# Three PEER query tiles computed from tokens x weight, with 1/rms applied to their scores

## The chip, the cores and the metric

The kernel runs on one core of a Trainium2 chip. The metric is the device time of one execution in microseconds (us). The engines named below are TensorE (PE, with its weight loads as PEld), VectorE (DVE), ScalarE (ACT), GpSimd (POOL) and SyncE (SP, which here issues most of the DMAs). Each engine works off its own list of instructions in order, and waits on semaphores for the others.

## The reference, cut to what matters

Two transformer blocks are applied to 256 tokens of width 1024. The first has two gated feed-forward parts around a token mixer; the second has a hybrid mixer, a cross attention to 256 memory tokens, and a PEER feed-forward part, after which the result is normalised. All is float32. What the change touches is the start of the PEER part:

```python
def rmsnorm_2(x, w):
    y = x * lax.rsqrt(jnp.mean(x * x, axis=-1, keepdims=True) + NORM_EPS)
    return y * w
...
x = x + memory_cross_attention(...)
x = x + peer_ffn(rmsnorm_2(x, norm_ffn_w), peer_wq, peer_sub_keys, peer_u, peer_v)
...
def peer_ffn(h, wq, sub_keys, u_table, v_table):
    q = (hf @ wq).reshape(t, PEER_HEADS, 2, PEER_HALF)        # 8 heads x 2 halves = 16 query tiles of 128
    sc = jnp.einsum('thpd,hpnd->thpn', q, sub_keys)           # 128 scores per token and tile
    top_v, top_i = lax.top_k(sc, PEER_TOPK)                   # the 16 best of each
    ... 16 best pairs of each head, softmax, and for the chosen experts gelu(u . h) times v
```

The kernel takes u . h for all 16,384 experts (128 tiles of 128, here called `pu`), and lets the gates choose.

## The kernel before, in words

Activations are kept transposed, as eight tiles of 128 features x 256 tokens: `hT` is the residual stream. A product in float32 is made of three fast products: weight and activation are each split into a rounded high part and the rest, and high x high, high x low and low x high are summed in PSUM. So each weight tile of 128x1024 (512 KB) goes through four steps in `Weights.chunk`: a DMA from SP into `raw` (L264), a cast on ACT into `whi` (L265), a subtraction on DVE that leaves `wlo` (L266), and 24 matmuls of 128x256 on PE (L192, the line of the helper that all matmuls share). `raw` has three buffers, `whi` and `wlo` two in each pool; in the PEER stage every third tile puts both parts into `wpair` instead (L266 there too), which takes over the place of `hT`.

The part in question runs as follows.

- The cross attention (`xa`) ends in its output projection, eight tiles of 24 matmuls on the moving operands `xoh` and `xol`; `ev_o` adds each to its part of `hT` (DVE, L1148).
- `norm_u` (L1154) then normalises: ACT squares each part of `hT` (L351), DVE adds the squares into `sqa` (L353), two matmuls with `mean` give the mean square of each token (`sm`), ACT takes the root (L362, with a table load ahead), DVE the reciprocal (L364), and `spread` makes of it a 128x256 tile that is the same on every partition: DVE writes two diagonal matrices `rd` (L372), PE multiplies them with ones. Then for each of eight parts DVE makes `nz` = hT x weight x 1/rms (L392), ACT casts it into `uh` (L273) and DVE leaves the rest in `ul` (L274).
- With `uh` and `ul` PE computes the sixteen query tiles (`pq`) and the first 24 of the 128 `pu` tiles, two query tiles and three `pu` tiles in turn (`weave`). `ev_q` takes a query tile out of PSUM into `qt` (ACT, L1206), loads its 128 keys (`ky`, SP, L1204), and computes the scores of the query tile before it (`scores`): two float32 matmuls of 128x128, a copy into `s1_` (ACT, L1219), and `top16` on DVE for each half of the tokens: MAX, MAX_INDEX, MATCH_REPLACE, MAX, MAX_INDEX (L1194 to L1198), ten instructions in all for a query tile.
- 36 `pu` tiles follow beside the choice of the pairs (`picks`), 68 beside the gates, and at last 128 steps with the `pv` tiles, where the weight tile is the moving operand in 512 columns.

A scheduler puts the instructions of each engine in one fixed order, by the order in which they were written and by its own estimate of when their inputs come; the pools set how far ahead a tile can be loaded. Small tiles called `edge` in the code place large tiles at chosen addresses; the pool `cp` lies ahead of all others in SBUF.

Of the kernel before, what the change touches and what calls it, by code (L numbers as in the profile page):

```python
# [12 lines left out]
F32 = mybir.dt.float32  # L13
F32R = mybir.dt.float32r
I32 = mybir.dt.int32
U32 = mybir.dt.uint32
AF = mybir.ActivationFunctionType
# [5 lines left out]
P = 128  # L23
T = 256
D = 1024
KD = 8
# [3 lines left out]
EPS = 1e-6  # L30
NEG = -1.0e30
NEXP = 128


_COLS = [
# [150 lines left out]
def body(tc, A, out):  # L186
    nc = tc.nc
    es = ExitStack()
    dve, act, pe, gp, sp = nc.vector, nc.scalar, nc.tensor, nc.gpsimd, nc.sync
# [4 lines left out]
    cp = es.enter_context(tc.tile_pool(name="cp", bufs=1))  # L194
# [18 lines left out]
    def col(name, j):  # L213
        o = _COFF[name][0] + j
        return cols[:, o:o + 1]
# [16 lines left out]
    def new_u():  # L232
        if first:
            return first.pop()
        return (cp.tile([P, KD, T], F32R, name="uh", tag="uh"),
                cp.tile([P, KD, T], F32R, name="ul", tag="ul"))
# [39 lines left out]
    def linear(*a):  # L276
        for _ in linear_steps(*a):
            pass
# [20 lines left out]
    def linear_steps(w, KT, ms, xh, xl, evac):  # L299

        per = 8 // KT if KT < 8 else 1
        for m0 in range(0, len(ms), per):
            grp = ms[m0:m0 + per]
            pss = [pmm.tile([P, 512], F32, name="mm", tag="mm") for _ in grp]
            for k0 in range(0, KT, 8):
                kn = min(8, KT - k0)
                if per > 1:
                    hi, lo = W.chunk(w[grp[0] // per], (per * KT, P))
                else:
                    hi, lo = W.chunk(w[grp[0], :, k0:k0 + kn, :], (kn, P))  # L310
                for g, m in enumerate(grp):
                    ps = pss[g][:, :T]
                    for k in range(kn):
                        kk = k0 + k
                        wh, wl = hi[:, g * KT + k, :], lo[:, g * KT + k, :]
                        mm(ps, wh, xh[:, kk, :], start=(kk == 0), stop=False)
                        mm(ps, wh, xl[:, kk, :], start=False, stop=False)
                        mm(ps, wl, xh[:, kk, :], start=False, stop=(kk == KT - 1))
            for g, m in enumerate(grp):
                evac(m, pss[g][:, :T])  # L320
            yield
# [24 lines left out]
    def sum_sq(pool, src, w=None):  # L346

        acc = pool.tile([P, T], F32, name="sqa", tag="sqa", bufs=2)
        for k in range(KD):
            sq = acc if k == 0 else pool.tile([P, T], F32, name="sq", tag="sq", bufs=2)  # L350
            act.activation(sq, src[:, k, :], AF.Square, scale=1.0 if w is None else w(k))  # L351
            if k:
                dve.tensor_tensor(acc, acc, sq, OP.add)  # L353
        ps = psm.tile([P, 512], F32, name="sm", tag="sm")
        for t in range(2):
            mm(ps[:, t:t + 1], acc[:, t * P:(t + 1) * P], mean)
        return ps[:, 0:2]

    def rsqrt(pool, ms):

        r = pool.tile([P, 2], F32, name="rr", tag="rr", bufs=4)
        act.activation(r, ms, AF.Sqrt, bias=epsc)  # L362
        r2 = pool.tile([P, 2], F32, name="rr2", tag="rr2", bufs=4)
        dve.reciprocal(r2, r)  # L364
        return r2

    def spread(pool, r):

        ps = psm.tile([P, 512], F32, name="sm", tag="sm")
        for t in range(2):  # L370
            d = pool.tile([P, P], F32, name="rd", tag="rd", bufs=2)
            dve.tensor_scalar(d, ident, r[:, t:t + 1], None, OP.mult)  # L372
            mm(ps[:, t * P:(t + 1) * P], ones, d)
        return ps[:, :T]

    def norm_u(pool, src, hi, lo, a, b):

        norm_apply(pool, src, spread(pool, rsqrt(pool, sum_sq(pool, src))), hi, lo, a, b)

    def scale_u(src, hi, lo, a):  # L380

        for k in range(KD):
            act.activation(hi[:, k, :], src[:, k, :], AF.Copy, scale=a(k))
            dve.scalar_tensor_tensor(lo[:, k, :], src[:, k, :], a(k), hi[:, k, :].bitcast(F32),
                                     OP.mult, OP.subtract)

    def norm_apply(pool, src, r, hi, lo, a, b):

        for k in range(KD):
            z = pool.tile([P, T], F32, name="nz", tag="nz", bufs=2)  # L390
            if b is None:
                dve.scalar_tensor_tensor(z, src[:, k, :], a(k), r, OP.mult, OP.mult)  # L392
            else:
                dve.tensor_tensor(z, src[:, k, :], r, OP.mult)
                z2 = pool.tile([P, T], F32, name="nz2", tag="nz2", bufs=2)
                act.activation(z2, z, AF.Identity, scale=a(k), bias=b(k))
                z = z2
            split(hi[:, k, :], lo[:, k, :], z)
# [706 lines left out]


    with tc.tile_pool(name="xa", bufs=1) as xp_:
        xK = xp_.tile([P, KD, T], F32, name="xK")
        xV = xp_.tile([P, 2, D], F32, name="xV")
        sp.dma_start(xK, kd)  # L1110
        sp.dma_start(xV, vd)

        uh, ul = new_u()
        scale_u(hT, uh, ul, lambda k: col("nxa", k))
        rq = rsqrt(npool, sum_sq(npool, hT))
        dve.tensor_scalar(rq, rq, 1.0 / 16.0, None, OP.mult)
        xq = xp_.tile([P, KD, T], F32, name="xq")
        edge(xp_, 192)
        xoh = xp_.tile([P, KD, T], F32R, name="xoh")
        xol = xp_.tile([P, KD, T], F32R, name="xol")  # L1120

        def attend(h):
            pst = [psm.tile([P, 512], F32, name="sm", tag="sm") for _ in range(2)]
            for t in range(2):
                ps = psm.tile([P, 512], F32, name="sm", tag="sm")
                for e in range(2):
                    mm(ps[:, :T], xq[:, 2 * h + e, t * P:(t + 1) * P], xK[:, 2 * h + e, :], start=(e == 0), stop=(e == 1))
                lg = xp_.tile([P, T], F32, name="xlg", tag="xlg", bufs=2)
                act.activation(lg, ps[:, :T], AF.Copy, scale=rq[:, t:t + 1])
                softmax_rows(xp_, lg, T, "x")  # L1130
                for kt in range(2):
                    pe.transpose(pst[kt][:, t * P:(t + 1) * P], lg[:, kt * P:(kt + 1) * P], ident)
            pt = xp_.tile([P, 2, T], F32, name="xpt", tag="xpt", bufs=2)
            for kt in range(2):
                act.copy(pt[:, kt, :], pst[kt][:, :T])
            for e in range(2):
                ps = psm.tile([P, 512], F32, name="sm", tag="sm")
                o = h * 256 + e * P
                for kt in range(2):
                    mm(ps[:, :T], xV[:, kt, o:o + P], pt[:, kt, :], start=(kt == 0), stop=(kt == 1))  # L1140
                split(xoh[:, 2 * h + e, :], xol[:, 2 * h + e, :], ps[:, :T])

        for h in range(4):
            linear(A["xa_q"], KD, [2 * h, 2 * h + 1], uh, ul, lambda m, ps: act.copy(xq[:, m, :], ps))
            attend(h)

        def ev_o(m, ps):
            dve.tensor_tensor(hT[:, m, :], ps, hT[:, m, :], OP.add)  # L1148

        linear(A["xa_o"], KD, list(range(8)), xoh, xol, ev_o)  # L1150


    uh, ul = new_u()
    norm_u(npool, hT, uh, ul, lambda k: col("nffn", k), None)  # L1154
    hd = dr.tile([P, KD, T], F32, name="hd")
    act.dma_start(hd, hT)
    W.pools = [wa]
# [29 lines left out]
    with tc.tile_pool(name="sel", bufs=1) as sp_:  # L1187
# [2 lines left out]

        def top16(s, v, ix, n):

            s2 = sp_.tile([P, n], F32, name="s2", tag=f"s2{n}", bufs=2)
            dve.max(v[:, 0:8], s)  # L1194
            dve.max_index(ix[:, 0:8], v[:, 0:8], s)
            dve.match_replace(s2, v[:, 0:8], s, -3.0e38)
            dve.max(v[:, 8:16], s2)
            dve.max_index(ix[:, 8:16], v[:, 8:16], s2)  # L1198
# [11 lines left out]
        def scores():  # L1210

            if not queries:
                return
            m, qt, ky = queries.pop()
            sc = psm.tile([P, 512], F32, name="sm", tag="sm")
            for t in range(2):
                mm(sc[:, t * P:(t + 1) * P], qt[:, t * P:(t + 1) * P], ky)
            s = sp_.tile([P, T], F32, name="s1_", tag="s1_", bufs=3)
            act.copy(s, sc[:, :T])  # L1219
            for t in range(2):  # L1220
                top16(s[:, t * P:(t + 1) * P], tv[t][:, m, :], ti[t][:, m, :], P)

# [78 lines left out]
                yield from pick_steps(t)  # L1301

        def q_steps():
            yield from linear_steps(A["pq"], KD, list(range(16)), uh, ul, ev_q)
            scores()

        weave(q_steps(), u_steps(0, NU1, u_ev), 2, 3)
# [92 lines left out]
```

## Time and profile before

| what | value |
|---|---|
| runs | 1742.51 us median of 3 (1738.4 to 1745.0) |
| profiled execution | 1747.64 us, of it a span of 1745.9 us from the first to the last instruction |
| mean granted TensorE clock | 0.990 of full speed |
| PE busy | 1679.2 us, 96% of the span |
| DVE busy | 1253.2 us, 72% |
| ACT busy | 1023.6 us, 59% |

Times inside the execution count from the start of the span. The kernel spends it in a chain of stages in which PE has little idle time; the transition from cross attention to PEER lies at 905 to 920 us, and the PEER part fills all that follows.

### The profile page before, as it was taken

What the parts mean: (1) busy time and instruction counts of PE and PEld (TensorE: products, weight loads), DVE (VectorE), ACT (ScalarE), POOL (GpSimd) and SP (SyncE); (2) the same over time, 40 slices, a digit from 0 to 9 for tenths busy, and PEclk for the clock granted to TensorE, in tenths of its full rate; (3) what the DMA queues carried; (4) which work ended last, traced back from release to release, by engine and by line L of the source; (5) the groups of instructions that cost most, each with busy time, mean ns of one, the idle gap of its engine ahead of it and who ended that gap; (6) DMA issues with size and microseconds to landing.
All of it is one profiled execution on the core that took longest, in us unless ns stands there. A gap on an engine that the chain in (4) does not pass through costs nothing.

```text
span 1745.9 us, 31700 instructions
## 1 busy us (share of the span) xinstructions
PE 1679.2 (96%) x12298; PEld 1575.6 (90%) x12298; DVE 1253.2 (72%) x2223; ACT 1023.6 (59%) x1977; POOL 4.0 (0%) x36
## 2 busy tenths in 40 slices
PE   2999999899999999899999999999999999999998
PEld 2998998799999999898889999999999888888886
DVE  7888677767855579757557789589999755555554
ACT  5655466565744458666645446588877544445444
POOL 0000000000000000000000000000000000000000
PEclk9999999999999999999999999999999999999999
DMA  9988689345866657216425555644444555555554
GB/s 334 342 307 312 204 291 326 122 134 184 288 205 191 182 185 234 87 38 209 142 76 191 183 180 174 203 145 146 145 135 143 190 193 195 194 174 192 195 194 138
DMA packets 97717, 336.34 MB, mean 193 GB/s; under 512 B 10988, under 2 KB 16541, under 8 KB 96926
## 3 DMA queue, kind: packets, MB, share of 16 engines
q1 hardware_dynamic: 94828, 330.63, 56.2%
q10 hardware_dynamic: 2738, 3.68, 0.6%
q8 instruction: 97, 1.59, 0.4%
q14 instruction: 54, 0.44, 0.1%
HBM read 329.02 MB, written 5.25 MB: 191 GB/s over the span
## 4 chain that ended last, share of the span: by engine, by line
PE 78%; DVE 12%; ACT 4%; issue 3%; DMA 2%; SPq 0%; DVEq 0%; ACTq 0%
PE mm L192 71%; PE sm L192 7%; DVE wlo L266 3%; DVE aw L1329 2%; ACT whi L265 1%; DMA wr<-in_w_ada 1%; DVE ac L820 1%; DVE wr L430 0%; DMA mnr<-in_rows 0%; DVE aw L1185 0%; DVE at L664 0%; DVE wpair L266 0%; DVE ul L274 0%; DMA xaV<-ke 0%; DVE ch L1285 0%
## 5 line engine op out<-in xcount | busy, mean ns | idle before, releaser
L266 DVE TENSOR_TENSOR wlo<-raw,whi 128x1024 fp32r<-128x1024 f32 (+1 forms) x448 | 543.1, 1214 | 250.5 <-ACT whi L265 249.9
L265 ACT CAST whi<-raw 128x1024 fp32r<-128x1024 f32 (+1 forms) x448 | 465.8, 1042 | 383.1 <-PE mm L192 270.1
L192 PE MATMUL mm<-uh,whi 128*128 128x256 f32 x2064 | 583.8, 285 | 9.8 <-ACT whi L265 7.4
L192 PE MATMUL mm<-ul,whi 128*128 128x256 f32 x2064 | 579.3, 281 | 2.7 <-DVE ul L274 2.2
L192 PE MATMUL mm<-uh,wlo 128*128 128x256 f32 x2064 | 578.3, 281 | 0.3 <-DVE wlo L266 0.2
L192 PEld LDWEIGHTS mm<-uh,whi 128*128 128x128 f32 x2064 | 391.4, 190 | 12.2 <-ACT whi L265 8.2
L192 PEld LDWEIGHTS mm<-ul,whi 128*128 128x128 f32 x2064 | 394.1, 191 | 4.4 <-DVE ul L274 2.7
L192 PEld LDWEIGHTS mm<-uh,wlo 128*128 128x128 f32 x2064 | 391.7, 190 | 2.1 <-DVE wlo L266 1.6
L266 DVE TENSOR_TENSOR wpair<-raw,wpair 128x1024 fp32r<-128x1024 f32 x90 | 110.2, 1224 | 80.6 <-ACT wpair L265 80.6
L192 PE MATMUL mm<-uh,wpair 128*128 128x256 f32 x768 | 143.8, 282 | 2.0 <-DVE wpair L266 1.7
L192 PE MATMUL mm<-whi,wh 128*128 128x512 f32 x344 | 134.0, 391 | 1.9 <-ACT wh L273 1.9
L192 PE MATMUL mm<-whi,wl 128*128 128x512 f32 x344 | 134.6, 391 | 0.0
L192 PE MATMUL mm<-wlo,wh 128*128 128x512 f32 x344 | 134.5, 391 | 0.0
L265 ACT CAST wpair<-raw 128x1024 fp32r<-128x1024 f32 x90 | 94.5, 1050 | 66.4 <-PE mm L192 65.3
L192 PEld LDWEIGHTS mm<-uh,wpair 128*128 128x128 f32 x768 | 119.9, 188 | 2.8 <-DVE wpair L266 2.3
L192 PE MATMUL mm<-wpair,wh 128*128 128x512 f32 x336 | 110.3, 389 | 0.0
L192 PE MATMUL mm<-ul,wpair 128*128 128x256 f32 x384 | 106.9, 278 | 0.0
L192 PE MATMUL mm<-hh,whi 128*128 128x256 f32 x352 | 99.2, 282 | 0.0
L192 PE MATMUL mm<-hl,whi 128*128 128x256 f32 x352 | 99.1, 282 | 0.0
L192 PE MATMUL mm<-hh,wlo 128*128 128x256 f32 x352 | 98.9, 281 | 0.0
L430 DVE SCALAR_TENSOR_TENSOR wr<-wr,cb 128x1024 f32<-128x1024 f32 x72 | 87.5, 1221 | 15.8 <-DMA wr<-in_w_ada 15.5
L192 PEld LDWEIGHTS mm<-whi,wh 128*128 128x128 f32 x344 | 64.6, 188 | 15.4 <-ACT wh L273 2.1
(838 smaller groups left out, 2631.7 us busy)
## 6 DMA issues: line engine op xcount, KB each, us to landing
raw<-in_pu SPq DMA_DIRECT2D x128, 512.0 KB, 3.3
raw<-in_pv SPq DMA_DIRECT2D x128, 512.0 KB, 3.3
raw<-in_ff_gu SPq DMA_DIRECT2D x88, 512.0 KB, 4.4
wr<-in_w_ada SPq DMA_DIRECT2D x72, 512.0 KB, 6.0
raw<-in_in_fm SPq DMA_DIRECT2D x34, 512.0 KB, 4.2
raw<-in_ff_dn SPq DMA_DIRECT2D x32, 512.0 KB, 3.7
raw<-in_in_tm SPq DMA_DIRECT2D x24, 512.0 KB, 4.9
raw<-in_in_gab SPq DMA_DIRECT2D x16, 512.0 KB, 3.7
```

What stands on the lines that cost most here:

```text
L192: pe.matmul(o, l, r, start=start, stop=stop)
L265: act.copy(hi[:, :n], raw[:, :n])
L266: dve.tensor_tensor(lo[:, :n], raw[:, :n], hi[:, :n].bitcast(F32), OP.subtract)
L430: dve.scalar_tensor_tensor(wr, wr, 1.0, cb, OP.mult, OP.mult, accum_out=mod[:, j:j + 1])
L820: dve.scalar_tensor_tensor(ac, xp[:, i:i + T], w(i), ac, OP.mult, OP.add)
L1329: dve.tensor_tensor(av[:, :, :nu], pv[:, :, :nu], av[:, :, :nu], OP.mult)
```

## The change

Three of the sixteen query tiles (`NQ0 = 3`) no longer wait for the norm. While the sum of squares is taken, `scale_u` writes `qh` and `ql`, the split of hT x weight without 1/rms: for each of the eight parts an ACT instruction (L384 after) and a DVE instruction (L385 after). They lie where the keys and values of the cross attention were (tags `xK` and `xV`). The first three `pq` tiles are multiplied with them. A copy of 1/rms is kept in a new tile `rc` (DVE, L1159 after), and the scores of these tiles are multiplied with it when they leave PSUM, in two ACT instructions of 128 columns in place of one of 256. The norm then follows as before for the other thirteen query tiles and all `pu` tiles. `ev_q` of the three early tiles stands first in `q_steps`. The scratch tile of `top16` has one tag for both of its widths. Lines after the first edit are one higher in the changed kernel, those of `top16` and later more.

```diff
+NQ0 = 3
...
-        xK = xp_.tile([P, KD, T], F32, name="xK")
-        xV = xp_.tile([P, 2, D], F32, name="xV")
+        xK = xp_.tile([P, KD, T], F32, name="xK", tag="xK")
+        xV = xp_.tile([P, 2, D], F32, name="xV", tag="xV")
...
-    uh, ul = new_u()
-    norm_u(npool, hT, uh, ul, lambda k: col("nffn", k), None)
+
+        qh = xp_.tile([P, KD, T], F32R, name="qh", tag="xK")
+        ql = xp_.tile([P, KD, T], F32R, name="ql", tag="xV")
+        scale_u(hT, qh, ql, lambda k: col("nffn", k))
+        rc = cp.tile([P, 2], F32, name="rc")
+        dve.tensor_copy(rc, rsqrt(npool, sum_sq(npool, hT)))
+        early = []
+        linear(A["pq"], KD, list(range(NQ0)), qh, ql, lambda m, ps: early.append((m, ps)))
+        uh, ul = new_u()
+        norm_apply(npool, hT, spread(npool, rc), uh, ul, lambda k: col("nffn", k), None)
...
-            s2 = sp_.tile([P, n], F32, name="s2", tag=f"s2{n}", bufs=2)
+            s2 = sp_.tile([P, P], F32, name="s2", tag="s2", bufs=2)[:, :n]
...
-            act.copy(s, sc[:, :T])
+            if m < NQ0:
+                for t in range(2):
+                    act.activation(s[:, t * P:(t + 1) * P], sc[:, t * P:(t + 1) * P], AF.Copy, scale=rc[:, t:t + 1])
+            else:
+                act.copy(s, sc[:, :T])
...
-            yield from linear_steps(A["pq"], KD, list(range(16)), uh, ul, ev_q)
+            for m, ps in early:
+                ev_q(m, ps)
+            yield from linear_steps(A["pq"], KD, list(range(NQ0, 16)), uh, ul, ev_q)
```

The lists of instructions are the same up to the transition. There, PE before goes from the last tile of the cross attention's projection (moving operand `xoh`) straight to the matmuls of the norm and then to the first query tiles on `uh`:

```order
L192 MATMUL mm_10521<-xoh_9867,wlo_10524 128x256
L192 MATMUL sm_10579<-mean_75,sqa_10556 128x1 x2
L192 MATMUL sm_10586<-rd_10587,ones_73 128x128
L192 MATMUL sm_10586<-rd_10590,ones_73 128x128
L192 MATMUL mm_10645<-uh_10554,whi_10647 128x256
L192 MATMUL mm_10680<-uh_10554,whi_10682 128x256
```

In the changed kernel 24 matmuls of the first early tile (mm_10603) and four of the second (mm_10634) stand between that projection and the mean:

```order
L193 MATMUL mm_10603<-qh_10553,wlo_10606 128x256
L193 MATMUL mm_10634<-qh_10553,whi_10636 128x256
L193 MATMUL mm_10634<-ql_10554,whi_10636 128x256
L193 MATMUL mm_10634<-qh_10553,wlo_10637 128x256
L193 MATMUL mm_10634<-qh_10553,whi_10636 128x256
L193 MATMUL sm_10595<-mean_75,sqa_10572 128x1 x2
L193 MATMUL mm_10634<-ql_10554,whi_10636 128x256
```

The rest of the second and the third early tile (mm_10665) follow, and only then the spreading of 1/rms, the first two scores, and the fourth and fifth query tile (mm_10806, mm_10859) on `uh`:

```order
L193 MATMUL mm_10665<-qh_10553,wlo_10668 128x256
L193 MATMUL sm_10698<-rd_10699,ones_73 128x128
L193 MATMUL sm_10698<-rd_10702,ones_73 128x128
L193 MATMUL sm_10766<-ky_10758,qt_10760 128x128 x2
L193 MATMUL sm_10788<-ky_10762,qt_10764 128x128 x2
L193 MATMUL mm_10806<-uh_10696,whi_10808 128x256
L193 MATMUL mm_10859<-uh_10696,whi_10861 128x256
L193 MATMUL mm_10806<-ul_10697,whi_10808 128x256
```

So three query tiles moved ahead of the norm on PE. On DVE, the split of the first `pu` tile (wpair_10734) before stands right behind the last `ul`, and the first `top16` behind three such splits:

```order
L274 TENSOR_TENSOR ul_10555<-nz_10617,uh_10554 128x256
L274 TENSOR_TENSOR ul_10555<-nz_10621,uh_10554 128x256
L266 TENSOR_TENSOR wpair_10734<-raw_10733,wpair_10734 128x1024
L266 TENSOR_TENSOR wlo_10766<-raw_10764,whi_10765 128x1024
L266 TENSOR_TENSOR wlo_10798<-raw_10796,whi_10797 128x1024
L1194 MAX tv0_10641<-s1__10718 128x8
```

In the changed kernel the last `ul` is followed by `top16` instructions; 34 of them, of the four query tiles with the scores s1__10769, s1__10791, s1__10844 and s1__10897, stand in one row, of which these are the first five:

```order
L275 TENSOR_TENSOR ul_10697<-nz_10733,uh_10696 128x256
L1209 MAX_INDEX ti0_10756<-tv0_10754,s2_10772 128x8
L1205 MAX tv1_10755<-s1__10769 128x8
L1205 MAX tv0_10754<-s1__10791 128x8
L1206 MAX_INDEX ti1_10757<-tv1_10755,s1__10769 128x8
L1207 MATCH_REPLACE s2_10778<-tv1_10755,s1__10769 128x128
```

At the end of that row comes the split of the first `pu` tile (now wpair_10913), and those of the next two between the last `top16` instructions:

```order
L1206 MAX_INDEX ti1_10757<-tv1_10755,s1__10897 128x8
L1209 MAX_INDEX ti0_10756<-tv0_10754,s2_10899 128x8
L1207 MATCH_REPLACE s2_10905<-tv1_10755,s1__10897 128x128
L267 TENSOR_TENSOR wpair_10913<-raw_10912,wpair_10913 128x1024
L1208 MAX tv1_10755<-s2_10905 128x8
L267 TENSOR_TENSOR wlo_10945<-raw_10943,whi_10944 128x1024
L1209 MAX_INDEX ti1_10757<-tv1_10755,s2_10905 128x8
L267 TENSOR_TENSOR wlo_10977<-raw_10975,whi_10976 128x1024
```

So on DVE the split has moved behind the choice of the best sixteen of four tiles. PE comes to the products with that split after the last matmuls of the fifth query tile (mm_10859) and a few of the first three `pu` tiles (mm_10911, mm_10942, mm_10974):

```order
L193 MATMUL mm_10859<-uh_10696,wlo_10862 128x256
L193 MATMUL sm_10894<-ky_10837,qt_10839 128x128 x2
L193 MATMUL mm_10911<-uh_10696,wpair_10913 128x256
L193 MATMUL mm_10911<-ul_10697,wpair_10913 128x256
L193 MATMUL mm_10942<-uh_10696,whi_10944 128x256
L193 MATMUL mm_10942<-ul_10697,whi_10944 128x256
L193 MATMUL sm_11040<-ky_10890,qt_10892 128x128 x2
L193 MATMUL mm_10974<-uh_10696,whi_10976 128x256
L193 MATMUL mm_10974<-ul_10697,whi_10976 128x256
L193 MATMUL mm_10911<-uh_10696,wpair_10913 128x256 x2
```

The tenth row is the first that reads the split. Apart from the order, `rc` takes 32 bytes of each partition in the pool `cp`, behind `uh` and `ul`, and every tile of the other pools begins 32 bytes further in the built program: `whi` at 55,648 where it was at 55,616, the `xoh` of the cross attention at 134,976 where it was at 134,944, the operand of the first feed-forward part's second product at 174,880 where it was at 174,848. `hT`, `uh` and `ul` stay.

## Rows read from the trace of the kernel before

**Rows 1.** The page: busy time of the engines (busy us, share of the span, instructions).

```profile
PE 1679.2 (96%) x12298; PEld 1575.6 (90%) x12298; DVE 1253.2 (72%) x2223; ACT 1023.6 (59%) x1977; POOL 4.0 (0%) x36
```

**Rows 2.** Busy time by windows from behind the transition to the end: the window, its length, then busy time and instructions of PE, PEld, DVE, ACT and POOL, the granted clock of PE (1.00 is 2.4 GHz, 0.50 is 1.2 GHz), DMA share and GB/s.

```profile
925.00:1040.00 115.00, 115.00 (x989) 115.00 (x988) 83.26 (x291) 55.74 (x93) 0.00 (x0) 1.00 0.55 183
1040.00:1060.00 20.00, 20.00 (x178) 20.00 (x177) 19.93 (x88) 12.91 (x18) 0.00 (x0) 1.00 0.55 182
1060.00:1100.00 40.00, 38.72 (x332) 37.92 (x331) 37.68 (x127) 24.62 (x37) 0.00 (x0) 1.00 0.57 187
1100.00:1380.00 280.00, 279.26 (x2426) 278.17 (x2424) 245.47 (x335) 208.36 (x545) 0.00 (x0) 1.00 0.44 149
1390.00:1740.00 350.00, 348.72 (x1555) 289.02 (x1553) 196.98 (x255) 172.03 (x260) 0.00 (x0) 1.00 0.56 186
```

**Rows 3.** Timeline of PE at the transition: start, duration, what, and in brackets the idle time before it and what ended it.

```profile
905.14 0.28 PE L192 MATMUL mm<-xoh,wlo 128*128 128x256 f32 x1
907.00 0.58 PE L192 MATMUL sm<-mean,sqa 128*128 128x1 f32 x4 [1.58 <-DVE sqa L353]
908.63 1.19 PE L192 MATMUL sm<-rd,ones 128*128 128x128 f32 x4 [1.06 <-DVE rd L372]
910.83 0.58 PE L192 MATMUL mm<-uh,whi 128*128 128x256 f32 x1 [1.01 <-ACT uh L273]
```

**Rows 4.** What PE waited for from 905 to 1110 us: us in total, times, longest.

```profile
PE sm L192 <- DVE sqa L353: 1.6, 1, 1.6
PE sm L192 <- DVE rd L372: 1.1, 1, 1.1
PE mm L192 <- ACT uh L273: 1.0, 1, 1.0
PE mm L192 <- DVE wpair L266: 1.0, 2, 0.8
PE mm L192 <- ACT whi L265: 0.5, 1, 0.5
```

**Rows 5.** Busy time of PE alone by windows, with its granted clock: the transition, and the stretches behind three longer waits of PE.

```profile
706.00:714.00 8.00, 6.76 (x23) 0.57 0.33 112
839.40:843.00 3.60, 3.48 (x17) 0.53 0.44 146
907.70:914.50 6.80, 4.86 (x21) 0.50 0.37 152
1385.60:1389.00 3.40, 3.40 (x9) 0.50 1.01 394
```

**Rows 6.** Timeline of PE: its waits ahead of such stretches, and one of 0.76 us that none follows until the next.

```profile
707.24 1.17 PE L192 MATMUL sm<-sq,band 128*100 128x256 f32 x2 [4.09 <-ACT sq L905]
...
838.27 0.74 PE L192 MATMUL mm<-uh,whi 128*128 128x256 f32 x4 [1.43 <-ACT uh L383]
...
1380.28 0.50 PE L192 MATMUL mm<-uh,wpair 128*128 128x256 f32 x2 [0.76 <-DVE wpair L266]
1385.00 1.62 PE L192 MATMUL mm<-whi,wh 128*128 128x512 f32 x4 [1.95 <-ACT wh L273]
```

**Rows 7.** Timeline of DVE at the transition: the last part of hT, the last two sums, the first and last `nz` and `ul`, the first splits, the first `top16` (MAX8 to the last FIND_INDEX8) and what follows it.

```profile
905.46 0.42 DVE L1148 TENSOR_TENSOR hT<-mm,hT 128x256 f32<-128x256 f32 x1 [0.31 <-PE mm L192]
906.42 0.43 DVE L353 TENSOR_TENSOR sqa<-sqa,sq 128x256 f32<-128x256 f32 x1 [0.54 <-ACT sq L351]
908.00 0.17 DVE L364 RECIPROCAL rr<-rr 128x2 f32<-128x2 f32 x1 [1.15 <-ACT rr L362]
909.86 0.87 DVE L392 SCALAR_TENSOR_TENSOR nz<-hT,cols,sm 128x256 f32<-128x256 f32 x2 [1.18 <-PE sm L192]
...
915.93 0.98 DVE L274 TENSOR_TENSOR ul<-nz,uh 128x256 fp32r<-128x256 f32 x2
917.44 1.23 DVE L266 TENSOR_TENSOR wpair<-raw,wpair 128x1024 fp32r<-128x1024 f32 x1 [0.53 <-ACT wpair L265]
...
921.60 0.48 DVE L1194 MAX8 tv<-s__10718 128x8 f32<-128x128 f32 x2
...
923.88 0.28 DVE L1198 FIND_INDEX8 ti<-tv,s 128x8 uint32<-128x128 f32 x1
924.08 1.21 DVE L266 TENSOR_TENSOR wpair<-raw,wpair 128x1024 fp32r<-128x1024 f32 x1
```

**Rows 8.** Groups of ACT by line and shape from 905 to 925 us: busy us, mean ns of one, idle before.

```profile
L362 ACT ACT_TABLE_LOAD x1 | 1.3, 1283 | 0.0
L1219 ACT COPY s__10718<-sm 128x256 f32<-128x256 f32 x1 | 0.4, 384 | 0.0
```

**Rows 9.** Timeline of SP, which issues the weight and key tiles (start and duration of the issue).

```profile
894.24 0.33 SPq L264 DMA_DIRECT2D raw<-in_pq  x1
896.85 8.32 SPq L264 DMA_DIRECT2D raw<-in_pu  x3
```

**Rows 10.** Timeline of PE: eight matmuls in a row on `xoh` and `xol` (start of the first and the last), and seven on `uh` and `ul`.

```profile
903.48 0.28 PE L192 MATMUL mm<-xoh,whi 128*128 128x256 f32 x1
...
904.31 0.28 PE L192 MATMUL mm<-xol,whi 128*128 128x256 f32 x1
...
1041.82 0.28 PE L192 MATMUL mm<-ul,whi 128*128 128x256 f32 x1
...
1042.50 0.28 PE L192 MATMUL mm<-ul,whi 128*128 128x256 f32 x1
```

## The prediction

> **What bounds the kernel now.** I read the page first: PE is busy for 96% of the span, DVE for 72% [rows 1]. PE is the bound nearly everywhere, so a change is worth what it takes from PE's idle and slow time, and it costs what it adds to it. Next come the windows behind the transition [rows 2]: from 925 us on PE is busy all the time (115.00 of 115.00, 279.26 of 280.00, 348.72 of 350.00), only between 1060 and 1100 us does it idle for 1.28 us. What PE loses or gains near 910 us therefore reaches the end whole; nothing behind it gives it back. One stretch has a second engine close to its limit: from 1040 to 1100 us DVE is busy 57.6 of 60 us.
>
> The timeline of PE at the transition shows what can be won [rows 3]: the last matmul of the projection starts at 905.14, the first on `uh` at 910.83. Take 0.12 us for the last one, and 5.57 us lie between, with three waits (1.58, 1.06, 1.01) and two small groups of norm matmuls. The table of waits adds 0.5 us for a cast [rows 4]. The granted clock adds a third item: from 907.70 to 914.50 it is 0.50, which is 1.2 GHz [rows 5]; the window holds 21 matmuls, four of them those on `rd`. The 17 others took 914.5 - 910.83 = 3.67 us. At the later rate (115.00 us / 989 = 0.116 us each [rows 2]) they take 1.97, so the slow clock costs 1.7 us. Altogether 5.57 + 0.5 + 1.7 = 7.7 us, of which some 1.2 us are the norm's own matmuls and stay. **No gain at this place can be over 6.5 us**, 0.37% of the time.
>
> **What fills the gap.** Three query tiles are 72 matmuls, 72 x 0.116 = 8.4 us, ready without the norm. They need `qh` and `ql` of the last part of hT, which DVE starts at 905.46 and ends at 905.88 [rows 7]. ACT's part takes about what a square takes (0.4 us), then comes, on DVE, the split of the third early tile (1.23 us) ahead of the last `ql` (0.43): about 908.0. PE starts the first early tile at 905.26 and reaches the last part 21 matmuls later, at 907.7: a wait of 0 to 0.4 us. The weights are there: `pq` was issued at 894.24 and three `pu` by 905.2 [rows 9]; in these slots three `pq` come now. The rest of the early split and the copy into `rc` (7 x 0.4 us on ACT, 7 x 0.43 and 0.2 on DVE) lie beside the projection; the sum of squares ends some 2 us later than at 906.85, near 908.7, root (with a table load of 1.28 us [rows 8]), reciprocal and `rd` near 910.5. All that is hidden by the second and third early tile, which last until about 914.3. The two scaled activations of 128 columns in place of one of 256 (0.384 us [rows 8]) cost at most a second 0.38 us for each of three tiles on ACT, which is 55.74 of 115 us busy here [rows 2]: nothing. The shared scratch tag and the key loads, moved ahead on SP, cost PE between 0 and 0.4 us at the third score; I put it into the small waits below.
>
> **What takes it away again.** The spreading of 1/rms stands behind the third early tile on PE: 914.3. The first `nz` follows 1.23 us after its start, as before (908.63 to 909.86 [rows 3, 7]), or a little less at full clock: 915.0 to 915.5. So the norm is not earlier but 5 us later than before, and everything that needs `uh` and `ul` with it: thirteen query tiles and all `pu`. PE waits for the first `uh` (0.8 us: `nz` 0.43 and cast 0.4, less the first two scores). DVE's list then holds a split and a MAX ahead of the first `ul`: another 1.2 us of PE's. The eight pairs of `nz` and `ul` took 909.86 to 916.91, 7.05 us, back to back [rows 7]; now one split (1.23) and four instructions of `top16` lie among them. A `top16` of ten took 921.60 to 924.08 = 2.48 us [rows 7], 0.25 each, so 7.05 + 1.23 + 1.0 = 9.3 us and the last `ul` ends at 923.1 (with some overlap) to 924.5. PE follows with small waits, 0.5 to 1.0 us in all.
>
> Then comes the place on which the prediction rests. Before, the split of the first `pu` tile followed the last `ul` directly. Now 34 instructions of `top16` stand ahead of it: 34 x 0.25 = 8.4 us, then the split, 1.2 us. It is ready at 932.5 to 934. PE needs it much sooner: it has a few matmuls of three `pu` tiles and two scores left (with 1.3 us of waits for the casts of the second and third, which come late from ACT since their `raw` buffers were freed late), and stands at the first product with the lower part at about 926.5. **It waits 6 us there**, behind work that nobody needs before the choice of the pairs.
>
> The sum against the same point of work: waits 0.8 + 1.2 + 0.5 + 1.3 + 6 = 9.8 us (up to 11.5), plus the norm's matmuls 1.2, less the 7.7 us of before: +3.3 to +5, I take **+4**.
>
> **The clock.** In this trace each wait of PE from 1.4 us up is followed by a stretch at a granted clock of about half: 4.09 us at 707, then 0.57 over 706 to 714; 1.43 us at 838, then 0.53; 1.95 us at 1385, then 0.50 [rows 5, 6]; waits of 0.76 us at 1380 [rows 6] are not. A wait of 6 us should bring one. If the whole stretch of 6.8 us falls on saturated PE, half of it is lost, 3.4 us less what lies inside the wait; where most falls into the wait, as before the change, 1.7; if it fell wholly inside, 0. I take **+2.5**, near the row at 707, whose wait is the longest.
>
> **Behind.** At 1040 to 1100 us DVE is nearly full. PE comes there later, but four `top16` are already done: bounds are -1.3 us (the idle time there vanishes [rows 2]) and +2 us (4 us late, less 2.4 us of DVE's slack). I take **+0.5**. Sum: 4 + 2.5 + 0.5 = +7.0. The profiled execution is 1747.64 us with 1.7 us outside the span; it lies 5.1 us above the median of 1742.5 to which I add: 1742.5 + 7 = **1749.5 us** (1744 to 1752.5 by the bounds 3.3 + 0 - 1.3 and 5 + 3.4 + 2).
>
> **Rival 1: the 32 bytes, slower still.** `rc` moves all tiles of later pools by 32 bytes. At the same full clock the trace has two rates: on `xoh`, which starts 32 bytes past a multiple of 64 (134,944), matmuls start 0.83 / 7 = 0.1186 us apart; on `uh`, at a multiple (26,880), 0.68 / 6 = 0.1133 [rows 10]. If the place of the streamed operand makes this difference, the change moves the operand of the first feed-forward part's second product (528 matmuls) and `whi` as it streams in the last stage (about 1032 of 512 columns) to the bad place, and `xoh` and the mixer's operand (192 each) to the good one: (528 + 1032 - 384) x 0.0053 = 6.2 us. Against it: `uh` itself shows both rates, since 925 to 1040 has 0.116 on average and 1040 to 1060 20 / 178 = 0.112 [rows 2]. It decides if over some 330 of these matmuls change their rate. It gives 1749.5 + 6.2 = 1755.7, with twice the effect 1762; the opposite sign, a gain, 1743.
>
> [...]
>
> **Rival 2: the gap is filled and nothing is late, faster.** If DVE got through the 34 instructions before PE needs the split, the 6 us wait and the slow clock behind it would vanish: 0.8 + 1.2 + 0.5 + 1.3 + 1.2 - 7.7 = -2.7, with the two casts in time -4: 1738.5 to 1740. For it: PE does get 8.4 us of ready work where it stood idle. Against it: DVE executes in its order, and the 34 would have to take some 2.4 us, 0.07 us each, where the trace has 0.25.
>
> **How the numbers follow.** The forecast has a chance of 0.50, rival 1 0.30, its opposite 0.08, rival 2 0.12. Half a per cent, about what a measurement of this kernel can tell from no change, is 8.7 us: 1733.8 to 1751.2. Faster than that: 0.04, from rival 2 or the opposite of rival 1 with more than I have found. Slower: three tenths of the forecast (0.15) and most of rival 1 (0.28), 0.43. Within: 0.53. The range runs from rival 2's lower end to the doubled rival 1, cut by a tenth on either side: 1739 to 1761.
>
> **What would show it.** In the profile after: PE without a wait from 905 to 914, the mean among the second early tile; `nz` first at 915; a row of MAX8 and FIND_INDEX8 on DVE from 924 to 932 and PE's wait of some 6 us for `wpair` at its end; a granted clock of 0.5 near 930. The forecast is wrong if that wait is under 3 us, or if the clock stays at 1.00 behind it. Rival 1 would show before 900 us, where the order is the same: the first block's end and the start of `xa` come later than in the trace of before by some microseconds, and the stage of `pv` is longer than its length of before.

## The result, and the profile after

The changed kernel takes 1761.22 us (median of 4 runs, 1757.24 to 1769.75) against 1742.34 us before: ratio 1.0108, 95% interval 1.0081 to 1.0135, which is slower by 18.9 us. The forecast was 1749.5 us with a range that ended at 1761; the direction was right and the size was not. The profiled execution of the changed kernel is 1769.75 us, its longest; its span of 1768.0 us is 22.1 us longer than the span before. Its busy times, to set beside [rows 1]:

```profile
PE 1701.3 (96%) x12298; PEld 1593.7 (90%) x12298; DVE 1255.2 (71%) x2232; ACT 1028.4 (58%) x1988; POOL 4.0 (0%) x36
```

PE is busy for 22.1 us more with the same 12298 instructions. So the lost time is not only idle time; some matmuls last longer. Where this happens is seen when the same PE instruction is looked up in both traces and its two start times are compared (instructions counted from the start up to 905 us, from the end behind it):

| place in the trace of before | start after, less start before |
|---|---|
| 140 us, first feed-forward part | +2.8 us |
| 470 us, ahead of the second feed-forward part | +4.7 |
| 572 us, behind its products on `uh` | +9.2 |
| 879 us, cross attention | +9.5 |
| 950 us, behind the transition | +13.5 |
| 1022 us | +14.0 |
| 1068 us, among the picks | +18.9 |
| 1375 us | +19.1 |
| 1421 us, start of the pv stage | +18.1 |
| 1738 us, its end | +22.2 |

Three things can be told apart. 9.5 us are there before the first changed instruction, and some 4 in the pv stage, where no instruction has moved either; the transition brings 4.0, and the PEER stage behind it 5.4, nearly all of it between 1022 and 1068 us. These are two single executions: in a second trace of the kernel before (e8 below) the instruction at 879 us starts 4.7 us earlier than in the first, so a place in this table holds to a few us only.

**The transition** went as forecast in kind. What PE waited for from 905 to 1130 us in the changed kernel (us in total, times, longest), to set beside [rows 4]:

```profile
PE mm L193 <- DVE wpair L267: 5.2, 1, 5.2
PE mm L193 <- DVE wlo L267: 2.1, 1, 2.1
PE mm L193 <- DVE ul L275: 1.0, 1, 1.0
PE mm L193 <- ACT whi L266: 0.5, 1, 0.5
PE mm L193 <- ACT uh L274: 0.3, 1, 0.3
```

The three waits of [rows 3] are gone; the early tiles fill that place. The timeline of PE (start, duration, in brackets the idle time before it), all of it some 9.5 us later than in the trace of before:

```profile
918.43 0.58 PE L193 MATMUL sm<-mean,sqa 128*128 128x1 f32 x4
924.09 0.61 PE L193 MATMUL sm<-rd,ones 128*128 128x128 f32 x4
924.53 1.06 PE L193 MATMUL sm<-ky,qt 128*128 128x128 f32 x8
925.89 0.39 PE L193 MATMUL mm<-uh,whi 128*128 128x256 f32 x1 [0.30 <-ACT uh L274]
...
941.96 0.80 PE L193 MATMUL mm<-uh,wpair 128*128 128x256 f32 x2 [5.16 <-DVE wpair L267]
```

The wait of 5.16 us ends with the split of the first `pu` tile. The timeline of DVE, to set beside [rows 7], shows what stood ahead of it:

```profile
924.74 0.87 DVE L393 SCALAR_TENSOR_TENSOR nz<-hT,cols,sm 128x256 f32<-128x256 f32 x2 [0.66 <-PE sm L193]
...
932.00 0.78 DVE L275 TENSOR_TENSOR ul<-nz,uh 128x256 fp32r<-128x256 f32 x2
932.70 0.08 DVE L1209 MATCH_VALUE_LOAD ti<-tv,s 128x8 f32 x1
...
940.49 0.27 DVE L1207 MATCH_REPLACE8 s<-tv,s__10897 128x128 f32<-128x128 f32 x1
940.69 1.22 DVE L267 TENSOR_TENSOR wpair<-raw,wpair 128x1024 fp32r<-128x1024 f32 x1
```

The row of `top16` lasts from 932.70 to 940.69, 8.0 us without a gap (8.4 forecast). The split does not need it: ACT's cast of the same tile had ended at 933.27. The clock fell with the wait (window, length, PE busy and matmuls, granted clock, DMA share, GB/s):

```profile
936.00:942.00 6.00, 0.55 (x3) 0.70 0.04 12
942.00:946.00 4.00, 4.00 (x22) 0.60 0.70 202
946.00:950.00 4.00, 4.00 (x37) 1.00 0.55 194
```

22 matmuls start from 942 to 946 us and 37 in the next 4 us: 15 x 0.108 = 1.6 us are lost behind the wait.

**The picks.** The wait of 2.1 us for `wlo` falls at 1057.51 us, with a slower clock near it (0.89 on average from 1050 to 1060). Before, this place had no wait [rows 4]. Wait and clock are some 3 us of the 4.9; the rest, by argument alone, is the rate, since PE started 178 matmuls in 20 us near there before [rows 2] and 86 or 87 in 10 us now. (e3 below, with the weights at their old place, loses 3 to 4 us in the same stretch.)

**The rate of matmuls.** Sixty microseconds in the middle of the second feed-forward part, all on `uh` and `ul`, at full clock, first in the trace of before and then in that of the changed kernel (window, length, PE busy and matmuls, clock, DMA share, GB/s):

```profile
480.00:540.00 60.00, 60.00 (x532) 1.00 0.61 203
```

```profile
480.00:540.00 60.00, 60.00 (x508) 1.00 0.57 190
```

60 / 532 is 0.113 us for each, 60 / 508 is 0.118. The instructions and their order are the same here; only the weight tiles lie 32 bytes further.

### The profile page after: what moved, and what is told of

It is laid out like the page before. It is cut to its first block, busy times and chain, and to the rows that moved or that the text cites. A ratio compares the mean times of both kernels' runs of the same rounds, so it can differ in the third digit from the quotient of the medians.

```text
span 1768.0 us, 31719 instructions
## 1 busy us (share of the span) xinstructions
PE 1701.3 (96%) x12298; PEld 1593.7 (90%) x12298; DVE 1255.2 (71%) x2232; ACT 1028.4 (58%) x1988; POOL 4.0 (0%) x36
## 5 line engine op out<-in xcount | busy, mean ns | idle before, releaser
L193 PEld LDWEIGHTS mm<-ul,whi 128*128 128x128 f32 x2048 | 389.7, 190 | 5.3 <-DVE ul L275 3.6
L266 ACT CAST wpair<-raw 128x1024 fp32r<-128x1024 f32 x89 | 93.5, 1050 | 68.8 <-PE mm L193 68.6
L193 PEld LDWEIGHTS mm<-uh,wpair 128*128 128x128 f32 x752 | 118.4, 190 | 6.7 <-DVE wpair L267 6.3
```

Of the source, the lines that this page charges most:

```text
L193: pe.matmul(o, l, r, start=start, stop=stop)
L266: act.copy(hi[:, :n], raw[:, :n])
```

## The experiments

Theory A at the start: two causes, the place of the weight tiles (rival 1) and the row of `top16` (the forecast). Theory B: only the order. Each kernel ran beside the kernel before on one chip; ratios are to those runs.

| run | place of the tiles | order | median us | ratio to before, 95% interval |
|---|---|---|---|---|
| the change | +32 bytes | row of 34 | 1761.22 | 1.0108 (1.0081 to 1.0135) |
| e1_pad32 | +32 | of before | 1755.08 | 1.0076 (1.0060 to 1.0093) |
| e2_pad64 | +64 | of before | 1757.85 | 1.0101 (1.0086 to 1.0116) |
| e3_same_place | of before | row of 34 | 1752.06 | 1.0065 (1.0052 to 1.0078) |
| e4_same_place_late | of before | top16 later | 1740.11 | 1.0000 (0.9982 to 1.0018) |
| e5_move_all | all tiles +32 | of before | 1742.36 | 0.9991 (0.9972 to 1.0010) |
| e6_move_uh_w | all but hT +32 | of before | 1747.94 | 1.0023 (0.9999 to 1.0047) |
| e7_new_place_late | +32 | top16 later | 1754.01 | 1.0064 (1.0042 to 1.0086) |
| e8_before_again | of before | of before | 1741.50 | one run |
| e9_late_no_bits | of before | top16 later, less work | 1733.99 | 0.9959 (0.9941 to 0.9977) |
| e10_before_no_bits | of before | of before, less work | 1741.55 | 1.0005 (0.9988 to 1.0023) |
| e11_minus32 | -32 | of before | 1753.47 | 1.0070 (1.0044 to 1.0096) |
| e12_late_pool | of before | e4, part on GpSimd | 1743.73 | 1.0012 (0.9995 to 1.0028) |

**e1 and e2: the place alone.** The empty tile behind `uh` and `ul` grows by 32 or 64 bytes (the one scratch tag of `top16` makes the room).

```diff
-    edge(cp, 64)
+    edge(cp, 96)      # e1; 128 in e2
-            s2 = sp_.tile([P, n], F32, name="s2", tag=f"s2{n}", bufs=2)
+            s2 = sp_.tile([P, P], F32, name="s2", tag="s2", bufs=2)[:, :n]
```

> The kernel before, with the space behind uh and ul enlarged by 32 bytes (and the one scratch tag of top16, which makes room for it), so that every tile of the later pools lies where the changed kernel has it; the order of work is that of before. Theory A (two causes: the place of the weight tiles changes the rate of matmuls, and DVE's order at the transition adds waits): slower than before by some 13 us, of which 4.8 us arise in the first feed-forward part on uh, 4.8 us in the second, and 3 to 4 us in the stage of pv; the transition as before. Theory B (all comes from the new order and the waits that it leads to): within 3 us of before. Theory C (the changed kernel's runs fell on slower runs): within 3 us.

> The kernel before with 64 bytes more behind uh and ul, order as before. If what counts is the place within 64 bytes (theory A1), the weight tiles keep it and the time is that of before within 3 us. If it is the place within a larger unit (A2), or any change of place, the rate of the uh stages changes here too: 5 to 15 us slower. Theory B: within 3 us.

e1 is 0.76% slower, 13 us, and e2 1.01%, 18 us (5 to 15 expected by A2), though no order changed: theory B falls. The same window as above, in e1:

```profile
480.00:540.00 60.00, 60.00 (x514) 1.00 0.59 193
```

That 64 bytes cost as much as 32 also drops A1: it is not the place within 64 bytes. Of the parts that the expectation for e1 names, the pv stage lost 4.1 us (3 to 4 expected). The two feed-forward parts (4.8 us each expected) can't be tested so: it turned out below that they run at either rate with every tile in its old place.

The scratch tag does more than make room: eleven small tiles of the picks lie 608 bytes lower in e1 and in the changed kernel, where the other tiles behind `rc` lie 32 higher. It is not the cause, since e5 has this tag and the time of before, and e11 below is slow without it.

**e3 and e4: the order alone.** `rc` goes into half of the empty tile, so that all else, apart from those eleven small tiles, lies as before; e4 also gives the `top16` of the first four query tiles a later priority.

```diff
-    edge(cp, 64)
+    edge(cp, 32)
...
-            for t in range(2):
-                top16(s[:, t * P:(t + 1) * P], tv[t][:, m, :], ti[t][:, m, :], P)
+            with later(LATE if m <= NQ0 else 0):       # e4, LATE = 300
+                for t in range(2):
+                    top16(s[:, t * P:(t + 1) * P], tv[t][:, m, :], ti[t][:, m, :], P)
```

> The changed kernel with 32 bytes less of empty space, so that rc lies in them and every tile that both kernels have lies where it lies before the change. Theory A: the 13 us of the place vanish, and what is left is the transition and the picks, 5 to 9 us slower than before. Theory B: as slow as the changed kernel, 17 to 20 us. Theory C: like before.

> As e3, and the top16 instructions of the first four query tiles have a later priority, so that 13 of them instead of 34 stand between the last ul and the splits of the first three pu tiles. If DVE's row of 34 is what PE waits for at the transition (theory A and the forecast), PE's wait of 5 us there falls under 2 us, and the time is 3 to 6 us below e3: between 2 us faster and 4 us slower than before. If the row is a symptom and the lateness comes from elsewhere (weights, casts), no faster than e3.

e3 is 0.65% slower (11 us, more than the 5 to 9 expected), e4 is level with before, as expected. In e3, PE waits from 900 to 960 us as in the changed kernel:

```profile
PE mm L193 <- DVE wpair L267: 5.2, 1, 5.2
PE mm L193 <- DVE ul L275: 1.0, 1, 1.0
PE mm L193 <- ACT whi L266: 0.5, 1, 0.5
PE mm L193 <- ACT uh L274: 0.3, 1, 0.3
```

and in e4:

```profile
PE mm L194 <- DVE ul L276: 0.7, 1, 0.7
PE mm L194 <- ACT uh L275: 0.3, 1, 0.3
```

The timeline of DVE in e4 has the split 0.8 us behind the end of the last `ul`:

```profile
920.98 0.75 DVE L276 TENSOR_TENSOR ul<-nz,uh 128x256 fp32r<-128x256 f32 x2
921.65 0.29 DVE L1209 MAX8 tv<-s 128x8 f32<-128x128 f32 x1
...
922.50 1.21 DVE L268 TENSOR_TENSOR wpair<-raw,wpair 128x1024 fp32r<-128x1024 f32 x1
```

So the row was what PE waited for. With it out of the way, the idea of the change works where it is applied: the same PE instructions, which start 1.3 us ahead of before at 854 us, start 5.7 us ahead at 950 us, a gain of 4.4. Yet the whole kernel is not faster.

**e5, e6 and e11: which place counts?** In e5 32 empty bytes lie ahead of `hT` and all tiles move together. In e6 they lie between `hT` and `uh`, so that `wpair` (in the place of `hT`) stays and all else moves. In e11 the weights move 32 bytes towards `uh`. (e5 and e6 have the scratch tag of e1, e11 does not.)

```diff
+    edge(cp, 32)       # e5
     hT = cp.tile([P, KD, T], F32, name="hT", tag="hT")
-    edge(cp, 192)
+    edge(cp, 224)      # e6
...
-    edge(cp, 64)
+    edge(cp, 32)       # e11
```

> The kernel before with 32 empty bytes ahead of hT instead of behind uh and ul: hT (and wpair with it), uh, ul and all weight tiles move together, and the distance between any stationary and any moving tile stays as before. Theory A3 (the rate of matmuls hangs on the place of the stationary tile against the moving one): like before within 3 us, uh on whi in the second feed-forward part at 113 ns. Theory A4 (it hangs on the place of the weight tiles by itself): as e1, 10 to 15 us slower, 118 ns there.

> The kernel before with the 32 bytes between hT and uh: uh, ul and the weight tiles move together, hT and wpair stay. Theory A3: uh on whi as before (113 ns in the second feed-forward part), but uh on wpair in the PEER stage and wpair on wh in the pv stage (before 115.3 and 226.7 ns) slower, near 118 and 233; 4 to 8 us slower than before. Theory A4: uh on whi at 118 ns, as in e1.

> The kernel before with 32 bytes less behind uh and ul: the weight tiles lie 32 bytes nearer to uh than before, order as before. If only the old distance gives the fast rate (or if any move off it costs), uh on whi in the second feed-forward part goes from 113 to 118 ns and the time is 8 to 18 us above before, as in e1 and e2. If only moves away cost, like before within 3 us.

From each trace I took the mean time between the starts of consecutive matmuls at full clock (ns). The first name in a row is the stationary operand (loaded by PEld), the second the moving one (streamed by PE):

| stationary on moving (stage) | before | change | e1 | e2 | e3 | e5 | e6 | e11 |
|---|---|---|---|---|---|---|---|---|
| whi on uh (second feed-forward part) | 113.0 | 118.7 | 117.2 | 118.4 | 113.0 | 117.5 | 114.0 | 118.4 |
| whi on uh (PEER) | 115.2 | 118.4 | 118.3 | 118.6 | 115.8 | 116.3 | 114.6 | 118.5 |
| wpair on uh (PEER) | 115.3 | 114.1 | 114.2 | 114.5 | 115.6 | 116.3 | 118.3 | 116.9 |
| wh on wpair (pv, 512 columns) | 226.7 | 233.7 | 233.7 | 233.3 | 226.7 | 226.7 | 233.6 | 234.2 |
| wh on whi (pv, 512 columns) | 226.5 | 227.9 | 227.9 | 227.3 | 226.7 | 226.7 | 227.9 | 229.7 |

e11 is 0.70% slower, 12 us (8 to 18 expected). The columns follow the distance between the two operands, not the place of either. Where the weights moved and `uh` did not (change, e1, e2, e11), `whi` on `uh` is slow and `wpair` on `uh` less so or not at all (114 to 117). In e6 `whi` moves with `uh`, `wpair` stays, and it is the other way round. In the pv stage `wpair` stays while `wh` moves (change, e1, e2, e6, e11): 233 to 234. In e5 every distance is as before, and so is the time (0.9991). A4 falls. For e6 it is the rates that show this: its time is 4 us above before (4 to 8 expected), with an interval that reaches 1. Not every number fits: in e11 `wpair` on `uh` and `wh` on `whi`, at their old distances, are slower too (116.9 and 229.7), which is open, and e5's second feed-forward part is at 117.5 where 113 was expected. The next run bears on that.

In the PEER part and the pv stage the traces of all runs separate without an exception. `whi` on `uh` (PEER) is at 114.6 to 116.3 in the nine traces at the old distance and at 118.2 to 118.6 in the five at a changed one; `wh` on `wpair` is at 226.5 to 226.8 in eight and at 233.3 to 234.2 in six. What it is in the distance that counts is not shown: -32, +32 and +64 bytes all cost.

**e8: the kernel before, profiled again.**

> The kernel before, unchanged, for a second profile. If its first feed-forward part on uh runs at one rate in each execution, it is 113 ns again, and the 118 ns of e3 there came from the change; if the rate can differ between executions with every tile in one place, it may be 118 here too. The waits at 905 to 920 us come back as 1.6, 1.1 and 1.0 us.

The waits came back as 1.6, 1.1 and 1.0 us. It has 113 ns in the first part on `uh`, as the first profile, but 118 in that part's second product, which was at 113. In e3 and e6, with `whi` as far from `uh` as before, the first part on `uh` was at 118; in e9 and e12 below, where the distance is the old one too, the second part was at 117, as in e5. So at the old distance a stage runs at either rate, from one execution to the next; at a changed one the `uh` stages of all five profiles (change, e1, e2, e7, e11) ran at 117 to 119. Why a rate is taken at the old distance is open.

**e7: the new place with the later top16.** The edit is e4's, with the empty tile at 64.

> The changed kernel with the later top16 of e4, but with rc where the change has it, so that the weight tiles lie 32 bytes further. If place and order are two causes that add: e4 plus what e1 lost, 12 to 16 us slower than before, 7 us faster than the changed kernel or more. If the slower matmuls hide the waits (or the reverse), the difference to the changed kernel is smaller than the 11 us between e3 and e4.

The ratio is 1.0064, some 11 us slower than before (12 to 16 expected) and 0.44% below the changed kernel, where the same step at the old place brought 0.65%. The place costs 0.64% with the later order and 0.43% with the row. The two causes, 0.76% and 0.65% by themselves, make 1.08% together; whether they overlap, as these numbers read, is within the intervals and was not settled.

**e9 and e10: where does e4's gain go?** Both leave out the steps in which the picks select an index bit by bit (so that other experts are chosen); e9 does so in e4, e10 in the kernel before.

```diff
                 n = 8
-                while n:
+                while n > 8:
```

> e4 with part of the work left out: the four steps per list in which the picks select the chosen index bit by bit (a bitwise AND and one or two predicated copies each, 36 DVE instructions in all with some 8 us) are not done, so that the indices of the experts are not the right ones. Theory D (e4 gains 5 us at the transition and loses most of it again near 1040 us, since DVE is full there and the lead runs into the row of the picks): PE's wait of 2.8 us there goes, and the kernel is 4 to 6 us faster than e10, which leaves out the same. Theory E (the lead is lost for another reason, such as weights or casts that come late): no faster than e10, within 2 us.

> The kernel before with the same steps of the picks left out. It has only 1.0 us of waits near 1078 us to lose with them: 0 to 3 us faster than before. Theory D: 4 to 6 us slower than e9. Theory E: like e9.

e10 is level with before, e9 0.41% faster, 7.6 us below e10 by the medians (4 to 6 expected). e4 waits once, 2.8 us, for a `wlo` between 1020 and 1110 us; e9 not over 0.3 us. In e4 the same PE instructions go from 7.0 us ahead of before at 1022 us to 1.5 us ahead at 1045 us; in e9 they keep the lead, 9.1 at 998, 9.0 at 1045, and 11.2 at 1093, where before has its own waits. Theory E falls: what the transition gains is lost at the picks, where a row of DVE work again stands ahead of a weight split. In e4 the clock falls with this wait:

```profile
1035.00:1040.00 5.00, 3.25 (x15) 3.25 (x16) 5.00 (x11) 1.62 (x3) 0.00 (x0) 0.61 0.41 122
1040.00:1045.00 5.00, 5.00 (x34) 5.00 (x34) 3.76 (x9) 1.33 (x2) 0.00 (x0) 0.71 0.57 198
```

49 matmuls fit into 8.25 us of busy time, where 72 would at 0.115 us each: some 2.6 us, which with the wait of 2.8 make up nearly all of the 5.5 us lost there. Theory D is right about the place, but not that the lead is what runs into the row. e3, which comes there 4 to 5 us later than before, waits as long between 1020 and 1110 us:

```profile
PE mm L193 <- DVE wlo L267: 3.1, 2, 2.8
```

The row belongs to the new order. In e3 and e4 5.9 and 6.0 us (18 DVE instructions) lie between the starts of two splits there; from 1005 to 1105 us the longest such stretch of the kernel before is 4.3 us, and e9 has 3.6 us at this place. The length by itself does not decide: e4 has 5.5 us between two splits at 1008.8 and no wait of PE. The windows of e10 and then of e9 there (PE, PEld, DVE, ACT, POOL busy, clock, DMA):

```profile
1020.00:1040.00 20.00, 20.00 (x176) 20.00 (x175) 17.77 (x78) 9.55 (x16) 0.00 (x0) 1.00 0.49 165
1040.00:1060.00 20.00, 20.00 (x174) 20.00 (x174) 19.25 (x95) 14.16 (x20) 0.00 (x0) 1.00 0.58 193
```

```profile
1020.00:1040.00 20.00, 19.69 (x169) 19.29 (x169) 19.40 (x91) 13.86 (x19) 0.00 (x0) 1.00 0.55 183
1040.00:1060.00 20.00, 20.00 (x175) 19.96 (x174) 15.53 (x54) 10.56 (x16) 0.00 (x0) 1.00 0.59 197
```

**e12: a shorter row.** Seven small operations for each half of the picks go from DVE to GpSimd, for instance:

```diff
-            dve.tensor_copy(lf_, lo3)
+            gp.tensor_copy(lf_, lo3)
```

> e4 with seven small operations of each half of the picks moved from DVE to GpSimd (two on the gates, five on the indices), so that the row of 18 DVE instructions near 1035 us loses some 1.3 us. By theory D PE's wait of 2.8 us there shrinks by up to 1.3 us: 1 to 3 us faster than e4, hardly to be told from before. If GpSimd's share of the chain is slow or it disturbs DVE, slower than e4 by up to 5 us.

A miss: 1.0012, and PE's wait grew from 2.8 to 4.3 us (5.6 us in two waits, from 1010 to 1110 us). The timeline of DVE shows why:

```profile
1024.80 1.21 DVE L268 TENSOR_TENSOR wlo<-raw,whi 128x1024 fp32r<-128x1024 f32 x1
1026.43 0.29 DVE L1279 SCALAR_TENSOR_TENSOR ge__12705<-hf,lf__12669 128x128 f32<-128x128 f32 x1 [0.42 <-POOL hf L1276]
1027.27 0.55 DVE L1283 TENSOR_TENSOR ab<-af,ge__12705 128x128 uint32<-128x128 f32 x1 [0.54 <-POOL af L1281]
...
1032.23 1.22 DVE L268 TENSOR_TENSOR wlo<-raw,whi 128x1024 fp32r<-128x1024 f32 x1
```

The row is shorter in DVE's own work and longer in time: DVE now waits within it for GpSimd, whose cast of `lf_` took 1.35 us (0.22 us on DVE in e4). From one split to the next 7.4 us pass, where e4 has 6.0. So at this place the time between two splits counts, and not DVE's load by itself.

## Why the prediction was wrong, point by point

- **What bounds the kernel, and the limit of the gain: right.** What was lost near 910 us came out at the end, and the lead that e4 won there (4.4 us) stayed below the 6.5 us.
- **The filled gap: right.** No wait of PE from 905 us up to the first `uh`; the mean stands among the second early tile.
- **The row of top16: right, with its size.** 8.0 us of row for 8.4, a wait of 5.2 us for 6. e3 and e4 show that the row is the cause, both ways: 5.2 us with it, none with four instructions there. The trace has DVE's instructions in the order of its list: the split started at 940.69, right behind the row that it does not depend on, 7.4 us after ACT's cast of the same tile had ended (933.27).
- **Transition and clock together: +6.5 forecast, +4.0 measured** between 879 and 950 us. Both parts were too large: PE's waits came to 7.0 us (0.3, 1.0, 0.5 and 5.2) for 9.8, and the clock behind them to about 1.6 us for 2.5.
- **The clock in GHz** [rows 2] is not read from a trace: a trace gives the granted clock as a share of full speed, and no run shows which frequencies these are. What it shows of before: at 0.50 matmuls of 256 columns on `uh` and `ul` start 0.213 us apart (911.89 to 914.45 us), and those of 512 columns in the pv stage 0.427 us (1386.89 to 1388.59 us), where at 1.00 these took 0.113 to 0.118 and 0.227 us. The forecast does not need the frequency: its 1.7 us follow from starts and from the later rate.
- **"Behind" was mis-sized.** I took +0.5 with +2 as upper bound; it was +5.4 up to 1068 us. The bound counted DVE's free time over 60 us (2.4 us), but PE waits for one split, and what delayed it was the row between it and the one before, 6.0 us in the new order. The rows there, and not only the load of the window, had to be read.
- **The step that failed is the sum 4 + 2.5 + 0.5: it has no term for the place of the tiles.** The 32 bytes stood beside it as rival 1, with a chance of 0.30, as an alternative to the forecast and not as an addend; they cost together with it. Alone the place costs 13 us (e1), where rival 1 added 6.2, and as much as the order (e3, 11 us). Both signs that the prediction named for it appeared: 9.5 us ahead of the first changed instruction and 4.1 us in the pv stage. That the total lies near rival 1's doubled end of 1762 is luck: that end is made of an order of 7 us, which cost 11, and an effect on other tiles.
- **Rival 1's mechanism was wrong in its tiles.** I looked at the place of the streamed operand within 64 bytes and named the first part's second product and `whi` in the pv stage as losers. The first of these ran at 113 in e1 and 118 in e8, either way; `whi` in the pv stage lost 1.4 of 226.5 ns. What lost were the products of `whi`, which moved, with `uh`, which did not, and of `wh` with `wpair` likewise. And my argument against it, that `uh` shows both rates by itself, was sound as an observation and no argument: at the old distance either rate occurs.
- **Rival 2 did not occur**; e9 shows what it asked for: with both rows out of the way, in a kernel that leaves out the bit steps, the change gains 7 us (4 to 10 by the interval).
- **Two readings.** "Each wait of PE from 1.4 us up" has an exception in the same trace: PE waits 1.41 us ahead of its instruction at 329.67 us, and the clock is 1.00 from 300 to 700 us. And the bounds add up to 1744.5 and 1752.9 us, not 1744 and 1752.5. Neither changes the forecast.

No version was found that beats both kernels: e4, the change with its row and its place mended, is level with before (0.9982 to 1.0018).

## What to carry to other kernels

A small tile that is added in an early pool moves all tiles behind it, and can change the distance between stationary and moving operands; here 32 bytes cost 13 us. Compare the addresses of the two built programs, and keep the distances, before a time is put down to the order of work. Work that is made ready earlier also moves up in the lists of other engines: look for what now stands ahead of the steps that feed the bound engine, and read the rows between two of these, not only the load of the engine; whether such a row makes a wait has still to be tried, since one of 6.0 us did here and one of 5.5 did not. What is won at one place can be lost at the next such row, as in e4.

## What the runs showed of the hardware that was not expected

- At full clock, matmuls of 128x256 followed one another at 113 or at 118 ns in the second feed-forward part, and those of 512 columns (`wh` on `wpair`) at 226.7 or some 233.5 ns. With the distance between the two operands changed by -32, +32 or +64 bytes, the products of `whi` with `uh` ran at 117 to 119 ns in all of five profiles.
- With the same distance, a stage can run at either rate from one execution to the next (the second product of the first feed-forward part: 113 and 118 ns in two profiles of the kernel before).
- Two casts of 128x128 from uint32 to float32, one after the other, took 1.35 and 0.29 us on GpSimd (e12), and 0.22 us each on DVE (e4).
